# Decay matrices with dt in the exponent and masks on GpSimd, and eight outer convolution taps as ScalarE products added on GpSimd, in a hybrid Conformer/SSD block

## The chip, the cores and the metric

The kernel runs on one core of a Trainium2 chip. The metric is the device time of one execution in microseconds, given as the median of several runs. Engines are named as in the profile: PE is TensorE's matmuls and PEld its weight loads, DVE is VectorE, ACT is ScalarE, POOL is GpSimd, SP is SyncE, whose queue issues all DMAs of this kernel. "L513" is line 513 of the kernel before.

## The reference, cut to what matters

One layer over 512 latent tokens of 1024 channels with a context prefix of 256 tokens. A modulated norm is projected at once into the inputs of two branches.

Branch A is a convolution module: a gated input u, a depthwise convolution of width 31 along grid rows of 64 tokens, LayerNorm, SiLU, a projection:

```python
u = glu[..., :CONV_DIM] * jax.nn.sigmoid(glu[..., CONV_DIM:])
u = dwconv(u.reshape(bsz * n_seg, seg_len, CONV_DIM), lp['conv_dw_w'], lp['conv_dw_b'])
u = jax.nn.silu(layernorm(u.reshape(bsz, l, CONV_DIM), ...))
```

Branch B is a bidirectional Mamba-2 scan with 32 heads of 64 channels in 8 groups, state 128, chunks of 128 tokens. Within a chunk, per head and direction:

```python
cum = jnp.cumsum(dts * a, axis=2)
xdt = x5 * dts[..., None]
seg = cum_t[..., :, None] - cum_t[..., None, :]
decay = jnp.exp(jnp.where(lower, seg, -jnp.inf))
cb = jnp.einsum('bcqgn,bckgn->bcgqk', cs_, bs)
y_diag = jnp.einsum('bcgrqk,bckgrp->bcqgrp', cb[:, :, :, None] * decay, xdt)
```

so the weight of token k in the output at token q is cb[q, k] * exp(cum_q - cum_k) * dt_k for k up to q (backward: from q on), and both directions are added. To this come the states that enter each chunk, decayed by exp(cum). The branches are gated, added and projected, and an MLP with squared ReLU follows.

## The kernel before, in words

Everything is kept channels by tokens, in tiles of 128 channels by 512 tokens, in float32. Each product runs in three passes over high and low parts: `load_w` (L99) brings a weight tile of 128x1024, ScalarE casts the high part (L105, whi), VectorE subtracts (L106, wlo), and `gemm` (L109) does 8 x 3 matmuls of 128x512 (L114 to L116). Raw and split weights have two buffers each.

The program is written as a list; a scheduler orders each engine's queue beforehand by priority (the place in the list) and its own estimate of when things are ready. `later(n)` moves what is traced inside back by n instructions, a negative n forward. On the chip each engine then runs its queue strictly in order.

First come the modulation vectors, the norms and the first products. `dt_part` (L294) finds dt and the running sums cf of dt * a for all heads at once (heads on partitions), exp(cf) (L339), writes both to DRAM (s_cf), and transposes the weights to the chunk's end wg, cf and dt to token-major wgT, cfT, dtT (L350 to L358).

Then follow the eight groups, each with `ssd(g)` beside the projections of the next group, `proj(g+1)`. In `xbc` the product is convolved with 5 taps (ScalarE L370, VectorE L374) and passed through SiLU (L384). `ssd` works thus:
- cps = B^T C for the four chunks (L442), and VectorE multiplies it by a lower and an upper triangle into two tiles cbm (L446).
- B and x are transposed to token-major; x times wgT gives xw (L470), from which the states hst are built (L485 to L498).
- Two halves j of two heads r each. For each head and direction d a DMA (L507) spreads cf and exp(cf) over all partitions into cfb (three buffers). ScalarE makes four pieces Relu(-cf + cfT) (L510, one for each chunk because the bias is a column) and one Exp(-x) over all 512 (L512). VectorE multiplies by cbm (L513). Forward, ScalarE scales the four pieces by dt (L517); backward, VectorE multiplies four pieces by dt and adds them to the forward tile M (L520). Cd = C * exp(cf) (L523) is GpSimd's, but VectorE's for the forward direction of the second head (`DECAYS_V`).
- 24 small products into yps (L532, L536): first the states by Cd, then x by M. VectorE finishes yt (L540, L541), a DMA stores it to s_y, and GpSimd adds up its squares (L548).

Beside groups 0 to 4 one tile of the convolution module runs (`GLU_AT`): `glu` makes the gated input sg (L557, L562), and `taps`, 650 instructions later in priority, does the middle tap with the bias on ScalarE (L569) and the 30 others as `scalar_tensor_tensor` on VectorE (L575), each o += w * shifted u over the tokens that exist; GpSimd adds the finished tiles up into cacc (L580). The last three tiles run behind the groups, then come the gates, the LayerNorm of conv (L644 to L657, results ch and cl), the branch projections, the output projection and the MLP.

Of the kernel before, what the change touches and what calls it, by code (L numbers as in the profile page):

```python
# [24 lines left out]
CK = 31  # L25

# columns of the packed per-channel vectors
# [8 lines left out]
# order of the input projection's 128-column tiles  # L36
# [20 lines left out]
def build(tc, xT, ctxT, cond, crow, wada1, wada2, vecs, hv, cst, w_in, w_co, w_so, w_o, w_1, w_2, outT):  # L57
    nc = tc.nc
    with ExitStack() as es:
# [8 lines left out]
        C = cp.tile([P, 4, P], F32, name="C")  # L68
        ident, ones, mask_f, mask_b = (C[:, i, :] for i in range(4))

# [15 lines left out]
        @contextmanager  # L86
        def later(n):
            """what is traced inside gives way to the next n instructions"""
            tc.cur_priority += n
            yield  # L90
            tc.cur_priority -= n

# [37 lines left out]
        def rsqrt_mean(ps, n, cnt, r=None):  # L130
            """1/sqrt(sum/cnt + EPS) of a sum broadcast over the partitions"""
# [18 lines left out]
        def rsqrt_rows(parts, n, cnt, pool, out=None):  # L150
            """the same of the sum of several tiles, found token by token and then spread over the partitions"""
# [40 lines left out]
        with tc.tile_pool(name="st", bufs=1) as st:  # L192
# [31 lines left out]
            # products of nothing: the tensor engine's clock halves when it idles  # L224
# [52 lines left out]
        nc.sync.dma_start(C[:, 2:], cst[:, 2:])  # L277
# [7 lines left out]
        H2 = 2 * HEADS  # L285
        cfT = cp.tile([P, NCH, H2], F32, name="cfT")
        dtT = cp.tile([P, NCH, H2], F32, name="dtT")
# [6 lines left out]
        def dt_part(ps, pc):  # L294
            conv = bigt("conv")
            # rows: heads forward, the same again, heads backward, the same again; the first of each hold
            # chunks 0 to 2, the second chunk 3 and the context
# [10 lines left out]
            # softplus: max(v, 0) + log1p(u), u = exp(-|v|), log1p(u) = 2 atanh(u / (2 + u))  # L308
# [13 lines left out]
            # running sums within the chunks and within the context, backward ones from the end  # L322
# [15 lines left out]
            nc.vector.tensor_tensor(wg, wg, dt_, ALU.mult)  # L338
            nc.scalar.activation(ecf, cf, AF.Exp)  # L339
# [5 lines left out]
            # step s: chunk s forward, chunk 3 - s backward  # L345
# [4 lines left out]
            for src, dst in ((wg, wgT), (cf, cfT), (dt_, dtT)):  # L350
# [36 lines left out]
        def xbc_first():  # L387
            """the first group's, all of x's part before ctx's"""
# [22 lines left out]

        yacc = acct("yacc")
        cacc = acct("cacc")

# [22 lines left out]
        def ssd(g, Bt, Ct, X, Z):  # L437
            ch = lambda t, c: t[:, c * P:(c + 1) * P]
            # B^T C of every chunk, for both directions
# [3 lines left out]
            cbm = []  # L443
            for m in (mask_f, mask_b):
                t = spool.tile([P, NCH, P], F32, name="cbm", tag=f"cbm{len(cbm)}", bufs=1)
                nc.vector.tensor_tensor(  # L446
                    t, cps.rearrange("p (c q) -> p c q", q=P), m.unsqueeze(1).broadcast_to([P, NCH, P]), ALU.mult)
                cbm.append(t)
            # B by token
# [6 lines left out]
            # x by token, and times what reaches the chunk's end  # L456
# [21 lines left out]
            # states that enter the chunks: step s is chunk s forward, chunk 3-s backward  # L478
# [20 lines left out]
            # outputs of the heads, two to a PSUM tile  # L499
            for j in range(2):  # L500
                yps = py.tile([P, T], F32, name="yps", tag="py")
                Ms, Cs = [], ([], [])
                for r in range(2):
                    for d in range(2):
                        hd = d * HEADS + 4 * g + 2 * j + r
                        cb_ = spool.tile([P, 2, T], F32, name="cfb", tag="cfb", bufs=3)
                        nc.sync.dma_start(cb_, s_cf[hd].unsqueeze(0).broadcast_to([P, 2, T]))  # L507
                        e = (spool if d else tp).tile([P, T], F32, name="e", tag="e" if d else "M", bufs=2 if d else 3)
                        for c in range(NCH):
                            nc.scalar.activation(  # L510
                                ch(e, c), cb_[:, 0, c * P:(c + 1) * P], AF.Relu, bias=cfT[:, c, hd:hd + 1], scale=-1.0)
                        nc.scalar.activation(e, e, AF.Exp, scale=-1.0)  # L512
                        nc.vector.tensor_tensor(e, e, cbm[d].rearrange("p c q -> p (c q)"), ALU.mult)  # L513
                        if d == 0:
                            M = e
                            for c in range(NCH):
                                nc.scalar.activation(ch(M, c), ch(M, c), AF.Copy, scale=dtT[:, c, hd:hd + 1])  # L517
# [47 lines left out]
        def taps(t, sg):  # L565
# [4 lines left out]
            for j in range(CK):  # L570
                d = j - CK // 2
                if d == 0:
                    continue
# [49 lines left out]
        for t in late:  # L623
            q = glu(t, tp, "e")
            with later(LATE_LATER):
                taps(*q)
# [250 lines left out]
```

## Time and profile before

| what | value |
|---|---|
| median of 3 runs | 1263.39 us |
| lowest and highest | 1263.3 and 1267.06 us |
| span of the profiled execution | 1264.2 us |
| PE busy | 1220.7 us (97%) |
| DVE busy | 953.7 us (75%) |
| ACT busy | 667.4 us (53%) |
| POOL busy | 108.9 us (9%), 74 instructions |
| mean granted TensorE clock | 0.991 |

The profile is one execution; its span is 0.8 us above the median of the timed runs. A group of instructions is one line, engine, operation and tile names, with count, busy time and mean duration; behind the second bar stands the engine's idle time just ahead of these instructions and what ended it. Durations on one engine overlap by some tens of ns from one instruction to the next. Matmul ends are modelled, so a waiting PE can look busy.

### The profile page before, as it was taken

To read this page: it belongs to the slowest core of one execution; us is meant where nothing else is said; L and a number is where in the kernel's file an instruction comes from. 1 tells how busy PE (TensorE), PEld (TensorE's weight loads), DVE (VectorE), ACT (ScalarE), POOL (GpSimd) and SP (SyncE) were. 2 spreads that over 40 slices of the span, in tenths; PEclk is the share of its full clock that TensorE was granted. 3 is DMA by queue.
4 is the path that set the end of the run, shared out by engine and by line. 5 is a ranking of instruction groups with operands and counts; after the bars stand their busy time and mean duration, and the time that the engine had idled before them with its cause. 6 is when DMAs were issued, how large, how long until landed. Compare 5 with 4: busy or idle time off the path is not lost.

```text
span 1264.2 us, 17493 instructions
## 1 busy us (share of the span) xinstructions
PE 1220.7 (97%) x6665; PEld 995.6 (79%) x6665; DVE 953.7 (75%) x1567; ACT 667.4 (53%) x1124; POOL 108.9 (9%) x74
## 2 busy tenths in 40 slices
PE   6998999999999899999999999999999999999997
PEld 3786778777787778787888877778998888888886
DVE  6797689999999999998999798885843343443444
ACT  4557888686776748868453452134431331331442
POOL 0001222121020302124000000000000000000000
PEclk8999999999999999999999999999999999999999
DMA  9424363343342424333363357964222333233332
GB/s 363 142 67 133 137 198 128 120 146 106 121 159 93 158 83 147 112 134 117 109 193 126 119 188 258 305 196 153 62 65 86 100 100 92 92 100 101 96 104 67
DMA packets 56260, 169.96 MB, mean 134 GB/s; under 512 B 6640, under 2 KB 9584, under 8 KB 56048
## 3 DMA queue, kind: packets, MB, share of 16 engines
q1 hardware_dynamic: 56176, 168.85, 41.0%
q8 instruction: 52, 0.85, 0.3%
q14 instruction: 32, 0.26, 0.1%
HBM read 162.27 MB, written 6.55 MB: 134 GB/s over the span
## 4 chain that ended last, share of the span: by engine, by line
PE 65%; DVE 20%; DMA 8%; issue 3%; ACT 3%; SPq 0%; POOL 0%; DVEq 0%; ACTq 0%; POOLq 0%
PE ps L114 20%; PE ps L115 19%; PE ps L116 19%; DVE conv L575 5%; DVE wlo L106 3%; DVE Xt L374 3%; DMA aw<-in_wada_dram 2%; DMA cfb<-s_cf 2%; PE yps L536 2%; PE yps L532 2%; PE sps L485 1%; DMA yr<-s_y 1%; DVE aw L675 1%; DMA raw<-in_w_dram 1%; ACT whi L105 1%
## 5 line engine op out<-in xcount | busy, mean ns | idle before, releaser
L105 ACT CAST whi<-raw 128x1024 fp32r<-128x1024 f32 x163 | 170.9, 1049 | 320.6 <-PE ps L115 291.5
L106 DVE TENSOR_TENSOR wlo<-raw,whi 128x1024 fp32r<-128x1024 f32 x163 | 203.8, 1251 | 84.3 <-ACT whi L105 76.1
L114 PE MATMUL ps<-hh,whi 128*128 128x512 f32 x632 | 258.0, 408 | 2.3 <-DVE Xt L374 2.1
L116 PE MATMUL ps<-hh,wlo 128*128 128x512 f32 x632 | 255.4, 404 | 2.3 <-DVE wlo L106 2.2
L115 PE MATMUL ps<-hl,whi 128*128 128x512 f32 x632 | 256.7, 406 | 0.0
L575 DVE SCALAR_TENSOR_TENSOR conv<-sg,V,conv 128x480 f32<-128x480 f32 (+14 forms) x240 | 173.3, 740 | 2.6 <-ACT conv L569 1.1
L114 PEld LDWEIGHTS ps<-hh,whi 128*128 128x128 f32 x632 | 119.4, 189 | 30.8 <-issue 7.2
L116 PEld LDWEIGHTS ps<-hh,wlo 128*128 128x128 f32 x632 | 119.4, 189 | 30.7 <-DVE wlo L106 4.7
L115 PEld LDWEIGHTS ps<-hl,whi 128*128 128x128 f32 x632 | 119.6, 189 | 26.5 <-issue 3.7
L711 DVE SCALAR_TENSOR_TENSOR x<-ps,mod,x 128x512 f32<-128x512 f32 (+1 forms) x48 | 31.7, 660 | 100.1 <-PE ps L116 100.1
L510 ACT ACTIVATE e<-cfb,cfT 128x128 f32<-128x128 f32 x256 | 83.9, 391 | 36.8 <-PE yps L532 17.5
L523 POOL TENSOR_TENSOR Cd<-Ct,cfb 128x512 f32<-128x512 f32 x48 | 72.6, 1518 | 313.0 <-DMA cfb<-s_cf 250.3
L116 PE MATMUL ps<-h2h,wlo 128*128 128x512 f32 (+1 forms) x240 | 89.8, 375 | 0.0
L115 PE MATMUL ps<-h2l,whi 128*128 128x512 f32 (+1 forms) x240 | 89.8, 375 | 0.0
L114 PE MATMUL ps<-h2h,whi 128*128 128x512 f32 (+1 forms) x240 | 89.4, 375 | 0.0
L115 PE MATMUL ps<-gl,whi 128*128 128x512 f32 x224 | 88.4, 395 | 0.0
L114 PE MATMUL ps<-gh,whi 128*128 128x512 f32 x224 | 88.2, 394 | 0.0
L116 PE MATMUL ps<-gh,wlo 128*128 128x512 f32 x224 | 87.9, 392 | 0.0
L374 DVE SCALAR_TENSOR_TENSOR Xt<-ps,V,Xt 128x255 f32<-128x255 f32 (+3 forms) x128 | 74.2, 605 | 3.9 <-ACT Xt L370 3.6
L114 PE MATMUL ps<-hc,whi 128*128 128x256 f32 x184 | 52.5, 285 | 3.1 <-DVE Xt L374 3.1
L115 PE MATMUL ps<-hc,whi 128*128 128x256 f32 x184 | 52.4, 285 | 0.0
L116 PE MATMUL ps<-hc,wlo 128*128 128x256 f32 x184 | 52.1, 283 | 0.0
(259 smaller groups left out, 2417.5 us busy)
## 6 DMA issues: line engine op xcount, KB each, us to landing
raw<-in_w_in_dram SPq DMA_DIRECT2D x81, 512.0 KB, 3.6
cfb<-s_cf SPq DMA_DIRECT2D x64, 512.0 KB, 4.4
raw<-in_w_dram SPq DMA_DIRECT2D x64, 512.0 KB, 3.5
aw<-in_wada_dram SPq DMA_DIRECT2D x64, 256.0 KB, 4.3
ablk<-in_wada_dram SPq DMA_DIRECT2D x16, 512.0 KB, 8.6
raw<-in_w_so_dram SPq DMA_DIRECT2D x16, 512.0 KB, 3.7
s_y<-yt SPq DMA_DIRECT2D x16, 256.0 KB, 2.2
yr<-s_y SPq DMA_DIRECT2D x16, 256.0 KB, 3.6
```

What stands on the lines that cost most here:

```text
L105: nc.scalar.copy(hi, raw)
L106: nc.vector.tensor_tensor(lo, raw, hi, ALU.subtract)
L114: nc.tensor.matmul(ps, lhsT=whi[:, k, :], rhs=rhi[:, k, t0:t1], start=start and k == 0, stop=False)
L115: nc.tensor.matmul(ps, lhsT=whi[:, k, :], rhs=rlo[:, k, t0:t1], start=False, stop=False)
L116: nc.tensor.matmul(ps, lhsT=wlo[:, k, :], rhs=rhi[:, k, t0:t1], start=False, stop=stop and k == KT - 1)
L374: nc.vector.scalar_tensor_tensor(o[:, lo:hi], ps[:, lo + d:hi + d], vcol(V_SCW + 5 * ch + j), o[:, lo:hi], ALU.mult, ALU.add)
L510: nc.scalar.activation(ch(e, c), cb_[:, 0, c * P:(c + 1) * P], AF.Relu, bias=cfT[:, c, hd:hd + 1], scale=-1.0)
L523: (nc.vector if (d, r) in DECAYS_V else nc.gpsimd).tensor_tensor(Cd, Ct, cb_[:, 1, :], ALU.mult)
L532: nc.tensor.matmul(o, lhsT=xt[:, c, hr, :], rhs=ch(Ms[r], c), start=False, stop=True, skip_group_check=True)
L536: nc.tensor.matmul(o, lhsT=hst[:, s, k, hr * 64:hr * 64 + 64], rhs=ch(Cs[k][r], c), start=k == 0 and c == 0, stop=False, skip_group_check= ...
L575: nc.vector.scalar_tensor_tensor(o[:, :, lo:hi], u[:, :, lo + d:hi + d], wv(j), o[:, :, lo:hi], ALU.mult, ALU.add)
L711: nc.vector.scalar_tensor_tensor(x1[:, j, a:b], ps[:, a:b], mod[:, gcol + j, 0:1], x1[:, j, a:b], ALU.mult, ALU.add)
```

## The change

Two edits.

*Decay matrices.* The two masked copies of cps go; one unmasked copy cb is made by ScalarE. The triangle is applied to the exponent: GpSimd's `affine_select` puts -1e30 into cfb (in place) where a token must not count, for each head and direction. dt moves into the exponent as ln(dt): `dt_part` forms bT = ln(max(dt, 1e-18)) - cf in place of cfT and dtT. Then four Exp pieces with bias bT give the finished decay times dt; Relu, the whole Exp and the scalings go. GpSimd adds the backward tile to the forward one, and VectorE multiplies the sum by cb once.

*Convolution.* The eight taps farthest from the middle, d = -15, 15, -14, 14, -13, 13, -12, 12, leave VectorE. For each, ScalarE makes the product w * shifted u into a tile `tap`, and GpSimd adds it to a tile `far`; the first product is written into `far` itself, the rest of which GpSimd sets to zero. When VectorE has done the other 22, GpSimd adds `far` to conv. While the groups run, `far` and `tap` have one buffer each; for the last three tiles they take the three buffers of the tags "Cd" and "M".

```diff
+FAR_TAPS = (0, 30, 1, 29, 2, 28, 3, 27)
+NEVER, DT_MIN = -1e30, 1e-18
+CFB = 3
...
-        C = cp.tile([P, 4, P], F32, name="C")
-        ident, ones, mask_f, mask_b = (C[:, i, :] for i in range(4))
+        C = cp.tile([P, 2, P], F32, name="C")
+        ident, ones = (C[:, i, :] for i in range(2))
...
-        cfT = cp.tile([P, NCH, H2], F32, name="cfT")
-        dtT = cp.tile([P, NCH, H2], F32, name="dtT")
+        bT = cp.tile([P, NCH, H2], F32, name="bT")
...
             nc.vector.tensor_tensor(wg, wg, dt_, ALU.mult)
+            nc.vector.tensor_scalar(dt_, dt_, DT_MIN, None, ALU.max)
+            nc.scalar.activation(dt_, dt_, AF.Ln)
+            nc.vector.tensor_tensor(dt_, dt_, cf, ALU.subtract)
             nc.scalar.activation(ecf, cf, AF.Exp)
...
-            for src, dst in ((wg, wgT), (cf, cfT), (dt_, dtT)):
+            for src, dst in ((wg, wgT), (dt_, bT)):
...
+        def far_tile(name):
+            if not at_end:
+                return spool.tile([P, T], F32, name=name, tag=name, bufs=1)
+            return tp.tile([P, T], F32, name=name, tag="Cd" if name == "far" else "M", bufs=3)
...
-            cbm = []
-            for m in (mask_f, mask_b):
-                t = spool.tile([P, NCH, P], F32, name="cbm", tag=f"cbm{len(cbm)}", bufs=1)
-                nc.vector.tensor_tensor(
-                    t, cps.rearrange("p (c q) -> p c q", q=P), m.unsqueeze(1).broadcast_to([P, NCH, P]), ALU.mult)
-                cbm.append(t)
+            cb = spool.tile([P, T], F32, name="cb", tag="cb", bufs=1)
+            nc.scalar.copy(cb, cps)
...
+                        x3 = cb_[:, 0, :].rearrange("p (c q) -> p c q", q=P)
+                        sign = -1 if d else 1
+                        nc.gpsimd.affine_select(x3, x3, pattern=[[0, NCH], [sign, P]], compare_op=ALU.is_ge,
+                                                fill=never, base=0, channel_multiplier=-sign)
                         for c in range(NCH):
                             nc.scalar.activation(
-                                ch(e, c), cb_[:, 0, c * P:(c + 1) * P], AF.Relu, bias=cfT[:, c, hd:hd + 1], scale=-1.0)
-                        nc.scalar.activation(e, e, AF.Exp, scale=-1.0)
-                        nc.vector.tensor_tensor(e, e, cbm[d].rearrange("p c q -> p (c q)"), ALU.mult)
-                        if d == 0:
-                            M = e
-                            for c in range(NCH):
-                                nc.scalar.activation(ch(M, c), ch(M, c), AF.Copy, scale=dtT[:, c, hd:hd + 1])
-                        else:
-                            for c in range(NCH):
-                                nc.vector.scalar_tensor_tensor(
-                                    ch(M, c), ch(e, c), dtT[:, c, hd:hd + 1], ch(M, c), ALU.mult, ALU.add)
+                                ch(e, c), cb_[:, 0, c * P:(c + 1) * P], AF.Exp, bias=bT[:, c, hd:hd + 1])
+                        es_.append(e)
...
+                    M = es_[0]
+                    nc.gpsimd.tensor_tensor(M, M, es_[1], ALU.add)
+                    nc.vector.tensor_tensor(M, M, cb, ALU.mult)
...
+            far = far_tile("far")
+            f = far.rearrange("p (r w) -> p r w", w=ROW)
+            for i, j in enumerate(FAR_TAPS):
+                d, lo, hi = span(j)
+                uj = u[:, :, lo + d:hi + d]
+                if i == 0:
+                    nc.gpsimd.memset(f[:, :, hi:] if d > 0 else f[:, :, :lo], 0.0)
+                    nc.scalar.activation(f[:, :, lo:hi], uj, AF.Copy, scale=wv(j))
+                    continue
+                q = far_tile("tap")
+                q = q[:, :8 * (hi - lo)].rearrange("p (r w) -> p r w", r=8)
+                nc.scalar.activation(q, uj, AF.Copy, scale=wv(j))
+                nc.gpsimd.tensor_tensor(f[:, :, lo:hi], f[:, :, lo:hi], q, ALU.add)
             for j in range(CK):
-                if d == 0:
+                if d == 0 or j in FAR_TAPS:
                     continue
...
+            nc.gpsimd.tensor_tensor(conv[:, t, :], conv[:, t, :], far, ALU.add)
```

More of the change, by code (lines that the diff above doesn't have):

```diff
@@ L276, in build @@
         nc.sync.dma_start(V[:, V_SNW:], vecs[:, V_SNW:])
-        nc.sync.dma_start(C[:, 2:], cst[:, 2:])
         c_k = lambda k: ctx[k // 2][:, k % 2, :]
@@ L410, in xbc_first @@
             return conv, Bt, Ct, [X0, X1]
+        def far_tile(name):
+            if not at_end:
+                return spool.tile([P, T], F32, name=name, tag=name, bufs=1)
+            return tp.tile([P, T], F32, name=name, tag="Cd" if name == "far" else "M", bufs=3)
+        at_end = []
         yacc = acct("yacc")
         cacc = acct("cacc")
+        never = nc.gpsimd.to_reg(NEVER)
         def proj(g):
@@ L503, in ssd @@
                 for r in range(2):
+                    es_ = []
                     for d in range(2):
                         hd = d * HEADS + 4 * g + 2 * j + r
-                        cb_ = spool.tile([P, 2, T], F32, name="cfb", tag="cfb", bufs=3)
+                        cb_ = spool.tile([P, 2, T], F32, name="cfb", tag="cfb", bufs=CFB)
                         nc.sync.dma_start(cb_, s_cf[hd].unsqueeze(0).broadcast_to([P, 2, T]))
+                        x3 = cb_[:, 0, :].rearrange("p (c q) -> p c q", q=P)
+                        sign = -1 if d else 1
+                        nc.gpsimd.affine_select(x3, x3, pattern=[[0, NCH], [sign, P]], compare_op=ALU.is_ge,
+                                                fill=never, base=0, channel_multiplier=-sign)
                         e = (spool if d else tp).tile([P, T], F32, name="e", tag="e" if d else "M", bufs=2 if d else 3)
@@ L568, in taps, with span @@
             wv = lambda j: vcol(V_DWW + t * CK + j)
+            def span(j):
+                d = j - CK // 2
+                lo, hi = max(0, -d), ROW - max(0, d)
+                return d, lo, hi
             nc.scalar.activation(conv[:, t, :], sg, AF.Identity, bias=vcol(V_DWB + t), scale=wv(CK // 2))
+            far = far_tile("far")
[11 more added lines that the diff above has]
+                nc.gpsimd.tensor_tensor(f[:, :, lo:hi], f[:, :, lo:hi], q, ALU.add)
             for j in range(CK):
-                d = j - CK // 2
-                if d == 0:
+                d, lo, hi = span(j)
+                if d == 0 or j in FAR_TAPS:
                     continue
-                lo, hi = max(0, -d), ROW - max(0, d)
                 nc.vector.scalar_tensor_tensor(
                     o[:, :, lo:hi], u[:, :, lo + d:hi + d], wv(j), o[:, :, lo:hi], ALU.mult, ALU.add)
+            nc.gpsimd.tensor_tensor(conv[:, t, :], conv[:, t, :], far, ALU.add)
             if t == 0:
@@ L621, in gate @@
             nc.scalar.activation(dst[:, t, :], ps, AF.Sigmoid)
+        at_end.append(True)
         for t in late:
@@ L837, in _layout @@
             inp["conv_dw_w"][0].reshape(CK, 8, P).transpose(2, 1, 0).reshape(P, -1)]
-    i = np.arange(P)
-    cst = np.stack([np.eye(P), np.ones((P, P)), i[:, None] <= i[None, :], i[:, None] >= i[None, :]], 1)
+    cst = np.stack([np.eye(P), np.ones((P, P))], 1)
     return {
```

## The prediction

> **What bounds the kernel now.** I read the page's totals first, then the busy time by stage, the matmul groups, and the chain of waits. The columns of the stage table are: stretch, PE (count), PEld, DVE, ACT, POOL, granted clock, DMA share, GB/s.
>
> ```profile
> span 1264.2 us, 17493 instructions
> ```
>
> ```profile
> 100.00:600.00 500.00, 483.13 (x2883) 388.14 (x2882) 457.88 (x748) 375.39 (x718) 100.58 (x66) 0.99 0.40 132
> 600.00:750.00 150.00, 149.82 (x659) 121.41 (x658) 137.10 (x197) 69.69 (x93) 8.14 (x4) 1.00 0.46 145
> ```
>
> The change lies in the stage from 100 to 600 us, where the eight groups of the state-space mixer run, and shortly behind it. There TensorE is recorded idle for 500 - 483.1 = 16.9 us, and VectorE is busy 457.9 of 500 us, that is 92%. In the next 150 us TensorE is full. The modelled ends of matmuls hide more waiting, so I compare one product in two stages:
>
> ```profile
> L114 PE MATMUL ps<-hh,whi 128*128 128x512 f32 x632 | 258.0, 408 | 2.3 <-DVE Xt L374 2.1
> ...
> L114 PE MATMUL ps<-h2h,whi 128*128 128x512 f32 x208 | 80.9, 389 | 0.0
> ```
>
> The same 128x512 pass takes 408 ns among the groups and 389 ns in the MLP, where nothing disturbs it. With 632 of each of three passes (taking the other two like this one) that is 3 x 632 x 0.019 = 36 us of waiting inside "busy". Together with the idle time some 16.9 + 36 = 53 us are the most that this stage can give back. Whom TensorE waits for is in the chain of waits over the same stage:
>
> ```profile
> by line: PE ps L114 13.7%; PE ps L115 13.6%; PE ps L116 13.4%; DVE conv L575 9.3%; DVE Xt L374 6.6%; DVE wlo L106 5.5%; DMA cfb<-s_cf 5.1%; PE yps L536 4.7%; issue 4.6%; PE yps L532 3.6%; PE sps L485 3.4%; DVE e L513 1.6%; DVE xw L470 1.4%;
> ```
>
> PE's own lines add up to 52.4%, so 47.6% is something else. VectorE's lines (conv, Xt, wlo, e, xw) are 24.4% of the stage, about half of that. Of the 53 us I put half, 27 us, down to a VectorE whose queue is full. This apportioning is the weakest step of the reading.
>
> **What leaves VectorE.** The next rows are groups by line: count, busy us, mean ns.
>
> ```profile
> L513 DVE TENSOR_TENSOR e<-e,cbm 128x512 f32<-128x512 f32 x64 | 46.6, 731 | 2.3 <-ACT e L512 2.3
> ...
> L520 DVE SCALAR_TENSOR_TENSOR e<-e,dtT 128x128 f32<-128x128 f32 x128 | 42.6, 358 | 0.2
> ...
> L446 DVE TENSOR_TENSOR cbm<-cps,C 128x512 f32<-128x512 f32 x16 | 10.4, 682 | 1.6 <-PE cps L442 1.4
> ```
>
> The mask products of B^T C (10.4 us), the mask product of each decay (46.6) and the multiply-adds with dt (42.6) go: 99.6 us. In their place each of the 32 pairs of a forward and a backward decay has one product with cb, of L513's shape: 32 x 0.731 = 23.4 us. The outermost taps are these:
>
> ```profile
> L575 DVE SCALAR_TENSOR_TENSOR conv<-sg,V,conv 128x408 f32<-128x408 f32 x16 | 12.6, 786 | 0.0
> ...
> L575 DVE SCALAR_TENSOR_TENSOR conv<-sg,V,conv 128x416 f32<-128x416 f32 x16 | 12.0, 749 | 0.1
> ...
> L575 DVE SCALAR_TENSOR_TENSOR conv<-sg,V,conv 128x400 f32<-128x400 f32 x16 | 11.7, 730 | 0.0
> ...
> L575 DVE SCALAR_TENSOR_TENSOR conv<-sg,V,conv 128x392 f32<-128x392 f32 x16 | 10.6, 661 | 1.2 <-ACT conv L569 1.1
> ```
>
> They sum to 46.9 us over eight channel tiles, 5.9 us for one. Five tiles belong to groups 0 to 4 (29.3 us), three run behind the groups (17.6 us). In the stage VectorE loses 99.6 + 29.3 - 23.4 = 105.5 us of its own work: 457.9 becomes 352.4 us, before what GpSimd adds.
>
> **What ScalarE gains and loses.** Here the columns are min/median/max ns and first and last start.
>
> ```profile
> L510 ACT ACTIVATE e<-cfb,cfT x256: 384/389/418, 112.3 to 601.0; 128x128 f32<-128x128 f32 x128
> ...
> L517 ACT ACTIVATE e<-e,dtT x128: 385/390/435, 119.4 to 600.4; 128x128 f32<-128x128 f32 x128
> L520 DVE SCALAR_TENSOR_TENSOR e<-e,dtT x128: 332/342/992, 123.4 to 604.6; 128x128 f32<-128x128 f32 x128
> L512 ACT ACTIVATE e<-e x64: 612/632/637, 115.3 to 602.0; 128x512 f32<-128x512 f32 x64
> L513 DVE TENSOR_TENSOR e<-e,cbm x64: 673/682/1783, 116.4 to 602.7; 128x512 f32<-128x512 f32 x64
> ```
>
> ```profile
> L613 ACT ACTIVATE yh<-yr,V 128x512 fp32r<-128x512 f32 x16 | 11.1, 724 | 11.6 <-DMA yr<-s_y 11.4
> ```
>
> The 256 pieces stay (Relu becomes Exp, the same form with a bias pointer); the 64 whole Exps (64 x 0.632 = 40 us) and the 128 scalings (128 x 0.390 = 50 us) go. New are eight copies of cps to cb (8 x 0.63 = 5 us) and 64 tap products. They are of L613's kind and somewhat narrower: at most 64 x 0.724 = 46 us, 40 of the 64 in the stage, 29 us. So ScalarE is relieved by 40 + 50 - 5 - 29 = 56 of 375 us, and costs nothing where it waits for nobody. Where it does wait is a rival below.
>
> **What GpSimd takes on.** First a row of how long its 128x512 add or product takes, then one encounter with VectorE.
>
> ```profile
> L523 POOL TENSOR_TENSOR Cd<-Ct,cfb x48: 1264/1304/3853, 112.4 to 594.0; 128x512 f32<-128x512 f32 x48
> ```
>
> ```profile
> 484.86 1.29 POOL L548 TENSOR_TENSOR yacc<-yacc,ysq 128x512 f32<-128x512 f32 x1 [7.49 <-ACT ysq L547]
> ```
>
> ```profile
> 484.76 0.75 DVE L374 SCALAR_TENSOR_TENSOR Ct<-ps,V,Ct 128x510 f32<-128x510 f32 x1
> 485.42 1.28 DVE L513 TENSOR_TENSOR e<-e,cbm 128x512 f32<-128x512 f32 x1
> ```
>
> An undisturbed GpSimd operation takes 1.29 us. In the stage there are 32 adds of the two decays (41 us) and for each of five tiles seven adds about 404 wide (1.29 x 404/512 = 1.02 us) and one of 512: 8.4 us, 42 in all. The 64 mask selections (one input, 128x512, on GpSimd) are in no row. A pass half as dear as the two-input one, 0.65 us, bounds them from below and two such passes, 2.6 us, from above; the nearest row says 1.29, which I take: 83 us. GpSimd goes from 100.6 to 100.6 + 41 + 42 + 83 = 267 us.
>
> The encounter shows the price. L513, median 682 ns, starts beside the GpSimd add, ends 0.55 us after it and takes 1.28 us; it reads two tiles of SBUF. The L374 ahead of it reads PSUM and one tile and keeps its 0.75 us beside the same add. How much such meetings cost in all is the mean against the median:
>
> ```profile
> L575 DVE SCALAR_TENSOR_TENSOR conv<-sg,V,conv 128x480 f32<-128x480 f32 (+14 forms) x240 | 173.3, 740 | 2.6 <-ACT conv L569 1.1
> ```
>
> ```profile
> L575 DVE SCALAR_TENSOR_TENSOR conv<-sg,V,conv x240: 613/684/1770, 198.0 to 706.0; 128x424 f32<-128x424 f32 x10, 128x480 f32<-128x480 f32 x10, 128x432 f32<-128x432 f32 x10, 128x472 f32<-128x472 f32 x9
> ```
>
> ```profile
> L523 DVE TENSOR_TENSOR Cd<-Ct,cfb 128x512 f32<-128x512 f32 x16 | 14.6, 910 | 7.6 <-DMA cfb<-s_cf 5.3 <-POOL Cd L523 1.4 <-issue 0.9
> ```
>
> L575: 240 x 0.056 = 13.4 us; L513: 64 x 0.049 = 3.1; L520: 128 x 0.016 = 2.0; L523 on VectorE, against L513's 682 ns: 16 x 0.228 = 3.6. That is 22 us over the stage's 66 GpSimd operations, 0.33 us each; the weight splits meet it too, and I take 0.4. New in the stage are 64 + 32 + 40 = 136 operations. The 96 of the decays get 0.4 us each (38 us); the 40 tap adds run while VectorE does the same tile's other taps, all of two SBUF inputs, and get 0.7, between 0.4 and their full 1.02: 28 us. VectorE's stage is then 352 + 66 = 418 us instead of 458, a relief of 40 us. The bounds are 352 + 136 x 0.33 = 397 and, with every new operation blocking for its whole length, 352 + 41 + 42 + 83 = 518 us.
>
> The Trainium skill, page "SBUF — State Buffer", section "SBUF: two separate sides", says that the port pair that VectorE and GpSimd share is an exclusive lock, held for the whole instruction, against VectorE instructions with two SBUF inputs. By that rule the upper bound is nearer than my 0.4 us, and it is the second rival; the encounter at 485 us agrees with it, the mean over 66 operations shows how seldom VectorE arrived just then.
>
> **The opening, and what is hidden.**
>
> ```profile
> 98.56 6.00 DMA s_dec<-dec
> 105.50 6.70 DMA cfb<-s_cf
> ```
>
> ```profile
> L512 ACT ACT_TABLE_LOAD x28 | 35.9, 1283 | 0.5
> ```
>
> Before the first decays the chain runs through the dt part and these DMAs. There the change adds a maximum, a logarithm with a table change (1.28 us, once or twice) and a subtraction, less one set of transposes; the first decay then waits for a selection (1.3 us). I charge 3 us (0 to 6). The three late tiles trade 17.6 us of taps for 24 GpSimd operations that VectorE may wait for, about 25 us at worst, so conv ends between 18 us earlier and 8 us later:
>
> ```profile
> L128 DVE TENSOR_TENSOR cl<-conv,ch x8: 684/685/686, 750.7 to 760.4; 128x512 fp32r<-128x512 f32 x8
> ```
>
> ```profile
> L114 PE MATMUL ps<-ch,whi x64: 387/389/396, 801.6 to 848.3; 128*128 128x512 f32 x64
> ```
>
> Its consumer starts 40 us after it is ready, so this costs nothing; only over 40 us late would it. Two fewer constant tiles and the shorter last step before the yps products (one product on VectorE in place of five instructions) I count at nothing beyond the sum.
>
> **The sum.** VectorE's share of the waiting is 27 us. A relief of 40 of 458 us leaves it 84% busy; I let two thirds of its waiting go, 18 us, against 3 us in the opening: -15 us. The profiled execution spans 1264.2 us and the median of the three timed runs is 1263.4 us, 0.8 us less; 1264.2 - 15 - 0.8 gives 1248 us.
>
> **Rivals.**
> 1. *More comes off.* ScalarE's relief counts too, its pieces no longer wait for VectorE (L517, L513), and 40 of the 53 us go: 1263 - 40 + 3 = 1226 us. For it: L513's and L517's steps lie on the path to every yps product. Against: 5.1% of the chain is the DMA of cfb, which stays.
> 2. *The lock eats the relief, slower.* Every new operation blocks VectorE for its whole length: 518 us of work in the stage. At the 96% that VectorE reached at best, that is 540 us, 40 longer: 1303 us. It decides from 106 / 136 = 0.78 us for each new operation, where VectorE is back at 458. For it: the encounter, and that sixteen taps or splits in a row leave no gap. Against: 0.33 us so far.
> 3. *GpSimd becomes the hop that is late, slower.* The decays of a pair now pass GpSimd twice in order, behind products that wait for cfb, and ScalarE's next tap product waits until GpSimd has taken the one before (one buffer), with weight casts and evictions queued behind it. On SyncE's queue a cfb load waits for its slot, and weight loads stand behind it:
>
> ```profile
> SPq L507 <- ACT e L510: 108.7, 33, 10.2
> ```
>
> The slot is now freed one selection later, 64 times 1.3 us on that queue. One operation of 1.5 us (1.29 and a short block) not hidden in each of the 16 half groups is 24 us: 1248 + 24 = 1272 us. With 2.6 us for a selection GpSimd has 351 us of its own work and this gets likelier.
> 4. *VectorE is relieved but was not what TensorE waited for*, or gain and hop cancel: 1263 us, within 0.3%.
>
> **How the numbers follow.** The forecast has 0.33, rival 1 0.21, rival 2 0.17, rival 3 0.17, rival 4 0.12. About 0.3% (4 us) is what a measurement of this kernel can tell from no change. Faster is 0.54, the same 0.12, slower 0.34. The forecast's own range is 1238 to 1258 (bounds of the blocking and of the opening). The range of 8 in 10 takes in rivals 1 and 3 and most of 2: 1222 to 1300 us.
>
> **What would show it.** Right: VectorE's stage at about 420 us busy, L575's mean still under 800 ns, the selections at 1 to 1.5 us, and the 128x512 pass nearer to 395 than 408 ns. Rival 2: means of two-input VectorE rows over 1 us. Rival 3: TensorE or ScalarE rows with a GpSimd releaser of tens of us. The sum is wrong if the stage shortens by under 5 us though VectorE falls to 420, which would be rival 4.

## The result and the profile after

The changed kernel takes 1309.28 us (median of four runs, 1307.22 to 1314.73) against 1265.22 us for the kernel before in the same session: a ratio of 1.0357, 95% interval 1.0329 to 1.0385 (the plain quotient of the two medians, 1.0348, lies inside it). It is slower by 44 us. The prediction was 1248 us, faster, with 1300 us as its upper end; it was wrong, in sign too.

In the kernel after, L118 to L120 are the three passes (L114 to L116 before), L109 and L110 the high and low weight parts, L380 the 5-tap convolution on VectorE, L602 the taps, L533 the product with cb, L525 ScalarE's decay pieces, L541 and L545 the yps products. The execution that was profiled is the longest of the four, 5 us above their median; the spans of the two profiles differ by 48.6 us. First the totals of the page:

```profile
span 1312.8 us, 17408 instructions
...
PE 1227.1 (93%) x6662; PEld 1008.3 (77%) x6662; DVE 918.8 (70%) x1329; ACT 644.7 (49%) x1012; POOL 285.5 (22%) x242
```

and the same two stages as before, with the same columns:

```profile
100.00:600.00 500.00, 458.79 (x2722) 378.70 (x2721) 406.32 (x520) 333.78 (x573) 243.07 (x204) 0.96 0.40 129
600.00:750.00 150.00, 132.64 (x620) 105.80 (x620) 122.25 (x139) 67.54 (x100) 42.02 (x33) 0.95 0.35 106
```

VectorE is down from 457.9 to 406.3 us, as intended. TensorE is busy 24 us less in the first stage (483.1 before) and 17 us less in the next (149.8), and the granted clock fell from 0.99 to 0.96 and from 1.00 to 0.95. All of the loss lies in and just behind these stages, as the first and last start of one product show, first in the kernel after, then in the kernel before:

```profile
L118 PE MATMUL ps<-hh,whi x632: 387/389/988, 38.4 to 756.5; 128*128 128x512 f32 x158
```

```profile
L114 PE MATMUL ps<-hh,whi x632: 387/389/798, 36.3 to 709.4; 128*128 128x512 f32 x158
```

The last of these products starts 47 us later; from there to the end of the span it is 556 us after and 555 before. Where the 47 us lie follows from the last output of a group (VectorE's yt, kernel after and kernel before):

```profile
L550 DVE TENSOR_TENSOR yt<-yt,Z x16: 681/1117/1780, 137.3 to 621.1; 128x512 f32<-128x512 f32 x16
```

```profile
L541 DVE TENSOR_TENSOR yt<-yt,Z x16: 673/683/1345, 140.7 to 607.8; 128x512 f32<-128x512 f32 x16
```

The groups end 13 us later, and the stretch from there to the last product grew by 34 us, from 102 to 135. Part of the 34 us is work: where TensorE waits among the groups, less of the later products (gates and last projections) is done there. The groups of instructions say who pays (count, busy us, mean ns, idle us ahead and its releasers):

```profile
L118 PE MATMUL ps<-hh,whi 128*128 128x512 f32 x632 | 264.8, 419 | 15.3 <-DVE Bt L380 13.8 <-ACT whi L109 1.4
...
L602 DVE SCALAR_TENSOR_TENSOR conv<-sg,V,conv 128x424 f32<-128x424 f32 (+10 forms) x176 | 168.4, 971 | 1.6
...
L533 DVE TENSOR_TENSOR e<-e,cb 128x512 f32<-128x512 f32 x32 | 32.3, 1026 | 12.5 <-POOL e L532 10.0 <-ACT cb L457 2.5
...
L597 POOL TENSOR_TENSOR far<-far,tap 128x400 f32<-128x400 f32 (+3 forms) x56 | 74.4, 1328 | 73.0 <-ACT tap L596 71.6
L529 POOL TENSOR_TENSOR Cd<-Ct,cfb 128x512 f32<-128x512 f32 x48 | 68.0, 1422 | 77.5 <-ACT Ct L390 77.5
L521 POOL TENSOR_SCALAR_AFFINE_SELECT cfb<-cfb 128x512 f32<-128x512 f32 x64 | 50.8, 794 | 135.3 <-DMA cfb<-s_cf 129.5
L532 POOL TENSOR_TENSOR e<-e 128x512 f32<-128x512 f32 x32 | 48.0, 1508 | 33.0 <-ACT e L525 32.9
```

The taps are the main reading. Before, 240 of them cost 173.3 us, 740 ns each; now 176 cost 168.4 us, 971 ns each. Sixty-four taps left VectorE and it got 5 us back. Their median has moved little (684 ns for 30 taps of a tile, now 725 for the wider 22): many run as before, others take twice as long. Which ones do follows from the trace when each tap is set beside what GpSimd ran at the time: the 74 taps that overlap no GpSimd operation take 0.70 us on average and none over 0.74, the 73 that overlap a tap add take 1.22.

```profile
L602 DVE SCALAR_TENSOR_TENSOR conv<-sg,V,conv x176: 650/725/1796, 182.3 to 719.2; 128x424 f32<-128x424 f32 x16, 128x432 f32<-128x432 f32 x16, 128x440 f32<-128x440 f32 x16, 128x448 f32<-128x448 f32 x16
```

The chain of waits over the group stage shows the same from TensorE's side:

```profile
by line: DVE conv L602 14.1%; PE ps L120 8.2%; PE ps L118 7.7%; PE ps L119 7.6%; issue 5.8%; DMA cfb<-s_cf 5.8%; ACT L525 3.9%; DVE wlo L110 3.9%; ACT e L525 3.6%; DVE Bt L380 3.5%; DVE yt L550 3.0%; ACT whi L109 3.0%; PE sps L494 3.0%; DVE
```

The three passes carry 23.5% of the chain, where it was 40.7%, and the taps 14.1%, where it was 9.3% with a third more of them: less of the chain runs over TensorE.

One place shows how. Timelines of the kernel after around 425 us (start, us, engine, instruction, count, idle time ahead), VectorE first, then GpSimd, ScalarE and TensorE:

```profile
420.33 6.86 DVE L602 SCALAR_TENSOR_TENSOR conv<-sg,V,conv 128x464 f32<-128x464 f32 x5
427.12 0.74 DVE L380 SCALAR_TENSOR_TENSOR Bt<-ps,V,Bt 128x510 f32<-128x510 f32 x1
427.78 1.26 DVE L602 SCALAR_TENSOR_TENSOR conv<-sg,V,conv 128x504 f32<-128x504 f32 x1
...
430.28 2.17 DVE L380 SCALAR_TENSOR_TENSOR Bt<-ps,V,Bt 128x511 f32<-128x511 f32 x4
```

```profile
421.79 1.29 POOL L557 TENSOR_TENSOR yacc<-yacc,ysq 128x512 f32<-128x512 f32 x1 [0.52 <-ACT ysq L556]
423.04 1.40 POOL L597 TENSOR_TENSOR far<-far,tap 128x408 f32<-128x408 f32 x1
425.19 1.47 POOL L597 TENSOR_TENSOR far<-far,tap 128x416 f32<-128x416 f32 x1 [0.76 <-ACT tap L596]
427.42 1.09 POOL L597 TENSOR_TENSOR far<-far,tap 128x416 f32<-128x416 f32 x1 [0.75 <-ACT tap L596]
```

```profile
424.47 0.65 ACT L596 ACTIVATE tap<-sg,V 128x416 f32<-128x416 f32 x1 [2.23 <-POOL far L597]
425.02 0.76 ACT L376 ACTIVATE Bt<-ps,V 128x512 f32<-128x512 f32 x1
```

```profile
428.75 0.39 PE L120 MATMUL ps<-hh,wlo 128*128 128x512 f32 x1
432.21 0.77 PE L118 MATMUL ps<-hh,whi 128*128 128x512 f32 x1 [3.07 <-DVE Bt L380]
```

Five taps take 6.86 us; at the median of 0.725 us they are 3.6 us. GpSimd's adds run beside them: four of the five taps end 0.50 to 0.53 us behind the end of a GpSimd add, and the one that begins between two adds takes 0.73 us. The two engines take turns. The eviction of Bt from PSUM is one step on ScalarE (L376) and four on VectorE (L380). The first L380, at 427.12, reads PSUM and one tile and keeps its 0.74 us, but it stands behind the taps in VectorE's queue, and the tap behind it takes 1.26 us beside the add at 427.42. The last of the four is in the group that starts at 430.28. ScalarE's step stands behind a tap product that waited 2.23 us for GpSimd to free `tap`. So two causes meet here, the blocked taps and ScalarE's wait. TensorE waits 3.07 us for the eviction. The first matmul after that wait takes 0.77 us, twice as long as those before it. A wait of the same length stands at 282 us:

```profile
281.66 0.76 PE L118 MATMUL ps<-hh,whi 128*128 128x512 f32 x1 [3.08 <-DVE Bt L380]
```

and windows around that place show TensorE's clock (last three columns: granted clock, DMA share, GB/s):

```profile
281.15:287.95 6.80, 6.05 (x14) 4.30 (x14) 6.80 (x11) 2.13 (x2) 0.00 (x0) 0.50 0.36 93
290.00:296.80 6.80, 6.80 (x43) 6.10 (x42) 6.03 (x8) 2.81 (x4) 2.94 (x2) 1.00 0.31 103
```

The wait of 3.08 us ends at 281.66 us, and in the 6.8 us around and behind its end TensorE is granted half its clock. By the clock column of the stage table, 0.04 x 500 + 0.05 x 150 = 27.5 us of clock is missing, against 0.01 x 500 = 5 us before. The difference, 22 us, is at most what the clock adds to the time, since part of the slow stretches would have been waiting anyway.

Behind the groups the taps of the last three tiles do the same to the weight splits. VectorE, then TensorE, kernel after:

```profile
670.13 6.07 DVE L602 SCALAR_TENSOR_TENSOR conv<-sg,V,conv 128x504 f32<-128x504 f32 x5
676.13 2.00 DVE L110 TENSOR_TENSOR wlo<-raw,whi 128x1024 fp32r<-128x1024 f32 x1
```

```profile
678.18 0.80 PE L120 MATMUL ps<-hh,wlo 128*128 128x512 f32 x1 [3.49 <-DVE wlo L110]
```

The list of waits of the kernel after (total us, times, longest) names both places, and the hop that ScalarE makes:

```profile
ACT tap L596 <- POOL far L597: 40.6, 27, 2.3
...
PEld ps L120 <- DVE wlo L110: 27.5, 19, 4.4
...
PEld yps L541 <- DVE e L533: 15.4, 7, 2.3
...
PE ps L118 <- DVE Bt L380: 13.8, 5, 3.1
```

### The profile page after: what moved, and what is told of

Read it like the earlier page. It is cut to its first block, busy times and chain, and to the rows that moved or that the text cites. A ratio compares the mean times of both kernels' runs of the same rounds, so it can differ in the third digit from the quotient of the medians.

```text
span 1312.8 us, 17408 instructions
## 1 busy us (share of the span) xinstructions
PE 1227.1 (93%) x6662; PEld 1008.3 (77%) x6662; DVE 918.8 (70%) x1329; ACT 644.7 (49%) x1012; POOL 285.5 (22%) x242
## 4 chain that ended last, share of the span: by engine, by line
PE 56%; DVE 22%; ACT 9%; DMA 8%; issue 3%; POOL 1%; SPq 0%; DVEq 0%; ACTq 0%; POOLq 0%
PE ps L120 18%; PE ps L118 18%; PE ps L119 17%; DVE conv L602 7%; DVE wlo L110 3%; DMA aw<-in_wada_dram 2%; DMA cfb<-s_cf 2%; ACT L525 1%; ACT e L525 1%; PE sps L494 1%; ACT whi L109 1%; DVE Bt L380 1%; DVE Xt L380 1%; DVE yt L550 1%; DVE aw L704 1%
## 5 line engine op out<-in xcount | busy, mean ns | idle before, releaser
L109 ACT CAST whi<-raw 128x1024 fp32r<-128x1024 f32 x163 | 170.7, 1048 | 293.6 <-PE ps L119 282.2
L110 DVE TENSOR_TENSOR wlo<-raw,whi 128x1024 fp32r<-128x1024 f32 x163 | 208.9, 1282 | 143.1 <-ACT whi L109 135.2
L118 PE MATMUL ps<-hh,whi 128*128 128x512 f32 x632 | 264.8, 419 | 15.3 <-DVE Bt L380 13.8
L120 PE MATMUL ps<-hh,wlo 128*128 128x512 f32 x632 | 263.5, 417 | 15.6 <-DVE wlo L110 15.6
L602 DVE SCALAR_TENSOR_TENSOR conv<-sg,V,conv 128x424 f32<-128x424 f32 (+10 forms) x176 | 168.4, 971 | 1.6
L120 PEld LDWEIGHTS ps<-hh,wlo 128*128 128x128 f32 x632 | 123.3, 195 | 50.0 <-DVE wlo L110 22.0
L118 PEld LDWEIGHTS ps<-hh,whi 128*128 128x128 f32 x632 | 123.9, 196 | 44.0 <-issue 15.5
L525 ACT ACTIVATE e<-cfb,bT 128x128 f32<-128x128 f32 x256 | 82.9, 392 | 21.2 <-POOL cfb L521 12.6
L597 POOL TENSOR_TENSOR far<-far,tap 128x400 f32<-128x400 f32 (+3 forms) x56 | 74.4, 1328 | 73.0 <-ACT tap L596 71.6
L120 PE MATMUL ps<-h2h,wlo 128*128 128x512 f32 (+1 forms) x240 | 89.8, 375 | 0.0
L118 PE MATMUL ps<-h2h,whi 128*128 128x512 f32 (+1 forms) x240 | 89.4, 375 | 0.0
L118 PE MATMUL ps<-gh,whi 128*128 128x512 f32 x224 | 88.2, 394 | 0.0
L120 PE MATMUL ps<-gh,wlo 128*128 128x512 f32 x224 | 87.9, 392 | 0.0
L529 POOL TENSOR_TENSOR Cd<-Ct,cfb 128x512 f32<-128x512 f32 x48 | 68.0, 1422 | 77.5 <-ACT Ct L390 77.5
L380 DVE SCALAR_TENSOR_TENSOR Xt<-ps,V,Xt 128x510 f32<-128x510 f32 (+3 forms) x128 | 74.3, 605 | 9.0 <-ACT Xt L376 8.4
L521 POOL TENSOR_SCALAR_AFFINE_SELECT cfb<-cfb 128x512 f32<-128x512 f32 x64 | 50.8, 794 | 135.3 <-DMA cfb<-s_cf 129.5
L532 POOL TENSOR_TENSOR e<-e 128x512 f32<-128x512 f32 x32 | 48.0, 1508 | 33.0 <-ACT e L525 32.9
```

The costliest lines, as they stand in the source:

```text
L109: nc.scalar.copy(hi, raw)
L110: nc.vector.tensor_tensor(lo, raw, hi, ALU.subtract)
L118: nc.tensor.matmul(ps, lhsT=whi[:, k, :], rhs=rhi[:, k, t0:t1], start=start and k == 0, stop=False)
L120: nc.tensor.matmul(ps, lhsT=wlo[:, k, :], rhs=rhi[:, k, t0:t1], start=False, stop=stop and k == KT - 1)
L380: nc.vector.scalar_tensor_tensor(o[:, lo:hi], ps[:, lo + d:hi + d], vcol(V_SCW + 5 * ch + j), o[:, lo:hi], ALU.mult, ALU.add)
L521: nc.gpsimd.affine_select(x3, x3, pattern=[[0, NCH], [sign, P]], compare_op=ALU.is_ge, fill=never, base=0, channel_multiplier=-sign)
```

## The experiments

Four theories were open. *Lock*: GpSimd's adds and VectorE's operations with two SBUF inputs exclude each other, and late evictions and splits follow. *Hop*: work stands on the path because it passes GpSimd in order (ScalarE's tap product that waits for the add, the add of the two decays ahead of the yps products). *Decay*: the decay part alone explains the loss. *Clock*: short waits of TensorE cost far more than their length because the clock halves behind them. In the expectations the lock is theory A, the hop of the two decays' add is B and later H, ScalarE's wait is C, a shortage of buffers for the forward decay is I, and the clock is K. Ratios are against the kernel before on the same chip; 0.1% is 1.3 us. The scheduler orders the queues anew for each version. By the traces run 3 has the order of the changed kernel on every engine, and run 8 on TensorE and GpSimd; in run 4 about a tenth of VectorE's instructions stand elsewhere, in run 5 about an eighth of TensorE's products against run 1. What a new order is worth by itself no run shows.

**1. The decay part alone.** All 30 taps back on VectorE.

```diff
-FAR_TAPS = (0, 30, 1, 29, 2, 28, 3, 27)
+FAR_TAPS = ()
-            far = far_tile("far")
...
-            nc.gpsimd.tensor_tensor(conv[:, t, :], conv[:, t, :], far, ALU.add)
```

> The decay part alone; all 30 taps stay on VectorE as in the kernel before. Theory A (the tap adds on GpSimd are the loss: they take turns with VectorE's taps, evictions and weight splits come late, TensorE waits and its clock is halved): 1255 to 1270 us, no wait of TensorE for VectorE's eviction of Bt, granted clock back at 0.985 or more. Theory B (the two decays' add on GpSimd is the late hop): 1290 to 1305 us, and TensorE still waits some 2.3 us for the product with cb in every group.

Measured: 1273.87 us, ratio 1.0094 (1.0069 to 1.0120). That is above the range of theory A and below that of B: the decay part is slower by itself, by 12 us, and the taps cost the rest: 1.0357 - 1.0094 = 2.6%, 33 us. Its group stage:

```profile
100.00:600.00 500.00, 467.48 (x2858) 388.13 (x2857) 425.81 (x574) 319.62 (x545) 205.25 (x162) 0.98 0.40 131
```

VectorE and ScalarE have 32 and 56 us less than before, and TensorE gets 16 us less done. Its waits:

```profile
ACT e L525 <- PE yps L541: 20.0, 7, 7.1
...
PEld yps L541 <- DVE e L533: 18.7, 7, 2.8
...
PE yps L541 <- DVE e L533: 15.7, 7, 2.4
```

and one of these places (GpSimd, VectorE, TensorE):

```profile
249.81 3.26 POOL L532 TENSOR_TENSOR e<-e 128x512 f32<-128x512 f32 x2 [9.10 <-ACT e L525]
```

```profile
251.89 1.73 DVE L533 TENSOR_TENSOR e<-e,cb 128x512 f32<-128x512 f32 x1 [1.17 <-POOL e L532]
```

```profile
253.68 1.09 PE L541 MATMUL yps<-e,xt 128*64 128x128 f32 x14 [2.39 <-DVE e L533]
```

ScalarE's pieces wait for a buffer that the earlier yps products still read; then two adds on GpSimd (3.26 us), then the product on VectorE (1.73 us beside a GpSimd operation), then TensorE, which had run out of other work. GpSimd's add is a link of that path. A wait of the same kind and length 72 us earlier has half the clock behind it; the one at 253.68 has not (TensorE's timeline at 181 us, then a window behind each):

```profile
181.37 1.97 PE L541 MATMUL yps<-e,xt 128*64 128x128 f32 x14 [2.39 <-DVE e L533]
```

```profile
181.00:187.80 6.80, 6.43 (x25) 5.14 (x26) 6.69 (x9) 1.91 (x5) 3.65 (x3) 0.51 0.18 66
253.70:260.00 6.30, 6.30 (x39) 5.29 (x40) 6.19 (x8) 2.13 (x6) 2.99 (x3) 1.00 0.17 66
```

Run 1 has five such waits of 2.39 us. Half the clock came with those that end at 181 and 397 us and not with those at 254, 325 and 469 us.

**2. The change without the 56 adds of far taps.** ScalarE still makes the products; seven of the outer taps are missing from the output.

```diff
-                nc.gpsimd.tensor_tensor(f[:, :, lo:hi], f[:, :, lo:hi], q, ALU.add)
```

> The changed kernel without the 56 adds of the tap products on GpSimd (seven of the eight outer taps are left out of the result); ScalarE's products, the last add and the 22 taps on VectorE stay. Theory A: all of the loss goes and VectorE's relief shows, 1235 to 1255 us, mean of a tap on VectorE back under 750 ns. Theory B: 1290 us or more.

Measured: 1268.43 us, 1.0035 (1.0015 to 1.0055). The adds on GpSimd are worth 1.0357 - 1.0035 = 3.2%, 41 us, though GpSimd was busy only 22% of the span. The relief itself didn't show as expected (1235 to 1255 us): against run 1 VectorE is busy 45 us less (877.8 in place of 923.2 us over the span), and the time falls by 0.6%, 7 us. The taps' row:

```profile
L601 DVE SCALAR_TENSOR_TENSOR conv<-sg,V,conv 128x424 f32<-128x424 f32 (+10 forms) x176 | 140.0, 810 | 1.6
```

Without the adds the 176 taps take 140.0 us in place of 168.4.

**3. The adds without ScalarE's wait.** The add reads u in place of `tap`, so the lock stays and ScalarE's products never wait for the adds; seven far taps go in unweighted.

```diff
-                nc.gpsimd.tensor_tensor(f[:, :, lo:hi], f[:, :, lo:hi], q, ALU.add)
+                nc.gpsimd.tensor_tensor(f[:, :, lo:hi], f[:, :, lo:hi], uj, ALU.add)
```

> The 56 adds stay on GpSimd but read the gated input in place of ScalarE's product (the result of the eight outer taps is wrong by that), so that ScalarE never waits for GpSimd. Theory A in the form that VectorE is blocked: still 1295 to 1312 us, taps on VectorE still over 900 ns. Theory C (ScalarE waits 41 us for its one product buffer, and evictions and weight casts queue behind): 1265 us or less.

Measured: 1301.56 us, 1.0324 (1.0297 to 1.0351). Nearly all of the loss stays; by the ratios, whose intervals overlap, the edit is worth 0.33%, 4 us. But it moves waits more than it takes them away:

```profile
ACT e L525 <- POOL cfb L521: 47.2, 9, 7.7
...
PEld yps L541 <- DVE e L533: 26.5, 7, 4.6
```

ScalarE's pieces wait 47.2 us for selections, where they waited 12.6 in the changed kernel, and TensorE waits 26.5 us for the product with cb in place of 15.4. In exchange its waits for Bt, 13.8 us in the changed kernel, are gone. So the waits at 282 and 432 us needed ScalarE's wait besides the blocked taps, and what that wait costs by itself stays open.

**4. The adds on VectorE.** The same sums; GpSimd keeps only the zeros of `far` and the last add to conv.

```diff
-                nc.gpsimd.tensor_tensor(f[:, :, lo:hi], f[:, :, lo:hi], q, ALU.add)
+                nc.vector.tensor_tensor(f[:, :, lo:hi], f[:, :, lo:hi], q, ALU.add)
```

> The 56 adds are VectorE's. It gets 56 x 0.64 = 36 us of work back, but nothing blocks it for a whole GpSimd add. Theory A: 1255 to 1275 us although VectorE has more work than in the changed kernel. If VectorE's own load decides: 1315 us or more.

Measured: 1278.39 us, 1.0142 (1.0113 to 1.0172). VectorE has 56 adds to make, and the kernel is 2.2%, 27 us, faster than with them on GpSimd, though 3 us above the expected range. ScalarE still waits for the adds, now for VectorE's:

```profile
ACT tap L596 <- DVE far L597: 30.1, 21, 3.1
```

```profile
L602 DVE SCALAR_TENSOR_TENSOR conv<-sg,V,conv 128x496 f32<-128x496 f32 (+10 forms) x176 | 141.9, 814 | 1.5
...
L597 DVE TENSOR_TENSOR far<-far,tap 128x400 f32<-128x400 f32 (+3 forms) x56 | 33.2, 593 | 0.0
```

An add costs VectorE 0.59 us. On GpSimd it costs 1.33 us there and (168.4 - 141.9)/56 = 0.47 us on VectorE's taps alone. So the taps' loss comes in the main from adds that run on GpSimd beside VectorE's taps: 27 us of it goes although ScalarE waits on (30.1 us, 40.6 before the edit). That the adds merely fill GpSimd's queue and make the decays late is not borne out, since TensorE's waits for the product with cb are no longer in the changed kernel than in run 1 (15.4 and 18.7 us). How much of the rest is ScalarE's wait, runs 2 to 4 don't separate.

**5 to 7. The path of the decay part.** On run 1: the add of the two decays on VectorE (5), a fourth buffer for the tag of M (6), both (7).

```diff
-                    nc.gpsimd.tensor_tensor(M, M, es_[1], ALU.add)
+                    nc.vector.tensor_tensor(M, M, es_[1], ALU.add)
```

```diff
-e = (spool if d else tp).tile([P, T], F32, name="e", tag="e" if d else "M", bufs=2 if d else 3)
+e = (spool if d else tp).tile([P, T], F32, name="e", tag="e" if d else "M", bufs=2 if d else 4)
```

> The decay part alone with the add of the two decays on VectorE in place of GpSimd. VectorE gets 32 x 0.69 = 22 us of work more than in the decay part alone (1273.9 us). Theory H (the add's hop over GpSimd makes the product with cb late, and TensorE waits 2.3 to 2.8 us for it in each group and loses clock behind it): 1257 to 1267 us, that wait under 1.5 us. If VectorE's load decides: 1275 to 1285 us.

> The decay part alone with four buffers in place of three for the forward decay tile. Theory I (the last head's Exps of a group start late since all three tiles wait for TensorE's products of the half before, so that all that follows lies on TensorE's path): 1255 to 1267 us, Exps no longer waiting for TensorE. Theory H: 1270 to 1276 us, unchanged.

> The decay part alone with both: the add on VectorE and four buffers. If H and I are both true: 1250 to 1262 us, the best so far. If only one is, as that one alone.

Measured: 1257.76 us, 0.9967 (0.9950 to 0.9983), for the add; 1264.83 us, 1.0024 (1.0012 to 1.0036), for the buffer; 1258.14 us, 0.9978 (0.9963 to 0.9993), for both. Moving the add turns the decay part from 0.9% slower to 0.3% faster, 16 us (the changed order of TensorE's products included), while VectorE gets more to do:

```profile
100.00:600.00 500.00, 478.05 (x2936) 396.10 (x2935) 441.26 (x625) 326.92 (x553) 156.50 (x131) 1.00 0.42 135
```

VectorE is at 441 us here and at 426 in run 1, and TensorE gets 11 us more done at full clock. The buffer is worth 9 us without that, and nothing on top of it, as if both shortened the same path.

**8. Far taps in the five tiles among the groups only.** The three late tiles keep all taps on VectorE.

```diff
+            FAR_TAPS = () if at_end else FAR_GROUPS
```

> The changed kernel with the eight outer taps on ScalarE and GpSimd for the five tiles beside the groups only; the three late tiles do all taps on VectorE. Theory A with the loss split by stage as the traces have it (the late stage waits 21 us more than the work left in it needs): 1285 to 1295 us. If the late stage only inherits a delay from the groups: 1303 us or more.

Measured: 1286.15 us, 1.0197 (1.0178 to 1.0216). Set against run 1 and the full change, the ratios split the loss, in this order of adding the parts: decay part 0.94% (12 us), far taps among the groups 1.03% (13 us), far taps in the three late tiles 1.60% (20 us). The second stage shows the last part:

```profile
600.00:750.00 150.00, 147.26 (x703) 119.46 (x702) 126.71 (x176) 63.45 (x86) 12.07 (x6) 0.99 0.40 123
```

TensorE is busy 147.3 us there at a clock of 0.99, against 132.6 at 0.95 with the late far taps.

**9 and 11. Keeping TensorE busy with zeros.** To price the clock by itself, run 1 got products with a zero weight tile ahead of the yps products that wait: 40 in each group (9), then 20 (11). They add nothing to the sums.

```diff
+ZEROS = 40
...
+        zero = cp.tile([P, 64], F32, name="zero")
+        nc.vector.memset(zero, 0.0)
...
+                    for i in range(ZEROS if k == 2 and j == 1 else 0):
+                        nc.tensor.matmul(yps[64 * (i % 2):64 * (i % 2) + 64, :P], lhsT=zero, rhs=ones,
+                                         start=False, stop=False, skip_group_check=True)
```

> The decay part alone, with 40 small products of zeros (64x128, some 2.2 us, adding nothing to the sums) in TensorE's queue just ahead of the last products of each group, where it waits 2.3 to 2.8 us for the product with cb. Theory K (besides the wait itself, the halved clock behind it is lost; the records show 13.7 us of it between 100 us and the end of the gates in the decay part alone, 3.4 us in the kernel before): the zeros fill the wait, the clock stays up, and 1263 to 1269 us come out against 1273.9 us although TensorE has 17 us more to do. If only the wait counts: 1273 to 1276 us. If the zeros come on top: 1285 us or more.

> As the run before with 20 products of zeros per group in place of 40: in that run the profile recorded 80 passes of 55 ns, 4.5 us per group and not 2.2, so that they overfilled the wait. 20 are 2.25 us, just the wait of 2.3 to 2.8 us in the decay part alone (1273.9 us). Theory K (the halved clock behind the wait is part of the price): 1262 to 1269 us. If only the wait counts: 1273 to 1276 us. If a product of zeros, wherever it stands, comes on top: 1290 us.

Measured: 1307.48 us, 1.0380 (1.0346 to 1.0413), and 1283.8 us, 1.0194 (1.0159 to 1.0229). A zero product is recorded as two passes of 55 ns, so 20 of them in eight groups add 18 us of TensorE time, 40 add 35. With 20 the group stage's clock is back at 0.99, against 0.98 in run 1:

```profile
100.00:600.00 500.00, 467.83 (x3044) 391.82 (x3042) 411.23 (x568) 314.19 (x537) 198.32 (x160) 0.99 0.40 130
```

Yet the kernel is 13 us slower than run 1 by the ratios (1.0194 and 1.0094), less than the 18 us added. TensorE's waits for the product with cb fell from 18.7 to 8.4 us. The clock theory, as priced in the expectations, failed: the filled waits were not worth what the fill cost. The zeros also changed the order of TensorE's other products, so the clock isn't isolated; how much of the half clock is a loss of its own remains open.

**10. What is left of the decay part.** Run 5 with a fourth buffer for cfb.

```diff
-CFB = 3
+CFB = 4
```

> The fastest so far (decay part alone, add on VectorE, 1257.8 us) with four buffers for cfb in place of three. If the loads of cfb still hold up the groups: 1248 to 1255 us. If not: 1256 to 1260 us, no difference.

Measured: 1252.76 us (1249.26 to 1256.33), 0.9932 (0.9910 to 0.9954): the fastest version, ahead of both kernels. The wait of SyncE's queue for a free cfb, in run 5 and then in this run:

```profile
SPq L517 <- ACT e L525: 94.2, 34, 8.2
```

```profile
SPq L517 <- ACT e L525: 80.4, 25, 7.6
```

It shrinks by 14 us only, so that the loads held up the groups agrees with the time but isn't shown step by step. A fourth buffer on the kernel before wasn't tried; so how much of the 0.7% is the new decay form and how much the buffer is told only by run 5, 0.3%, against this run, and their intervals touch.

## Why the prediction was wrong, point by point

**The loads were near.** Predicted for the group stage: VectorE 418 us, GpSimd 267. Measured: 406.3 and 243.1, in a stretch into which a little less of the work falls, since the groups end 13 us later. A selection, taken at 1.29 us, has a median of 0.638 us, just under the lower bound, and a mean of 0.79; four of the 64 take 1.5 to 1.7 us, each beside a weight split of VectorE. ScalarE was forecast 56 us lighter and is 42.

**The step that failed** is "A relief of 40 of 458 us leaves it 84% busy; I let two thirds of its waiting go, 18 us". VectorE fell by 52 us, to 81%, and the time rose by 44 us; the 128x512 pass, forecast nearer to 395 than to 408 ns, takes 419. A busy share says how much an engine has to do, not when it does it. What the runs show in its place: TensorE waits for particular instructions of VectorE (13.8 us for Bt evictions, 18.9 for weight splits, 12.6 for L533; in the kernel before 5.2 for the splits and none for Bt), and each of these got later: in a fixed queue a tap of 1.3 to 1.8 us delays the eviction behind it, however empty the queue is at other times. Run 5 shows it from the other side: 15 us more work on VectorE than in run 1, and 16 us less time. And run 2 against run 1 prices the relief without the tap adds on GpSimd: 45 us less on VectorE, 7 us of time, where the step counts 18 us for 40.

**Where blocking falls was averaged away.** I gave a tap add 0.7 us of blocking, and the size was fair, with 0.47 us measured on the taps alone. But the rows that I averaged came from GpSimd operations that rarely met VectorE. A dense row of taps beside a dense row of adds meets at every instruction, and that row stands in front of the evictions. The forecast that the taps' mean would stay under 800 ns failed: 971. It didn't follow from the sum either: 28 us of blocking on the 110 taps of the five tiles is 0.25 us each, on top of 740 ns. The total of the blocking was foreseen, and what it does to the order was not. The forecast's own range, 1238 to 1258 us, leaves out the upper bound of the blocking, 518 us, though it is said to rest on the bounds.

The Trainium skill, page "SBUF — State Buffer", section "SBUF: two separate sides", has this as an exclusive lock that the first comer of a VectorE operation with two SBUF inputs and a GpSimd operation that reads SBUF holds to its end. The five taps in 6.86 us, in turn with the adds, and the eviction from PSUM that kept its 0.74 us agree with it.

**"so this costs nothing", about the late tiles, was the largest single miss**, 20 us. I asked only who reads conv and found 40 us of slack. I didn't ask what else stands in VectorE's queue behind those taps: the weight splits of the last products, for which TensorE, full before, waited up to 4.4 us.

**Rival 2** (the lock) had the right mechanism and the wrong place: VectorE never came near 518 us, the blocked time hit the order and not the total. Its time, 1303 us, came nearest, but by luck, since the way there was another. **Rival 3** (the hop) was real as well: GpSimd's add of the two decays is worth 16 us (run 5, a new order of the queues included), near its 24, though that was worked out from 16 steps of 1.5 us and run 1 shows seven waits of at most 2.4 us; what ScalarE's wait for the tap adds costs stays open. I held these two for alternatives; they happened together, and that is how the time came out above the range. **Rivals 1 and 4** fell, since the time rose; what ScalarE's relief is worth no run shows by itself.

**The clock was not priced at all.** The forecast let a late VectorE cost TensorE its waiting time. The granted clock halved for some microseconds at the recorded waits of 3.08 and 3.07 us and at some of those of 2.39, and up to 22 of the 47 us could come from it. The Trainium skill, page "TensorE: Matmul & The Clock Gate", Part 1, gives an idle window of about 3.4 us as the condition and half rate as the result; the half rate agrees (0.50), but here a recorded wait of 2.39 us was enough in two of five places of run 1. As runs 9 and 11 failed to isolate it, its share remains open.

The opening, charged with 3 us, can be dismissed: by the two rows of yt, the first output of a group starts 3.4 us earlier than before (137.3 against 140.7).

## What to carry to other kernels

Before moving work from VectorE to GpSimd, ask whether VectorE does operations with two SBUF inputs at that time. Here it did, and the add was paid on both: 1.33 us on GpSimd and 0.47 on VectorE, against 0.59 us on VectorE alone, and the kernel was 27 us faster with the adds there. Before you turn a lighter engine into time, list the instructions of that engine for which the bottleneck waits, and ask of each whether it gets earlier or later. And look at everything queued behind a slowed row, not only at the reader of its result.

## What was not expected of the hardware

A GpSimd selection of 128x512 in float32 takes 0.638 us, half of its two-input add (1.29 us). A TensorE wait of 2.39 us at 181 us of run 1 came with half the clock for 6.8 us, and one of the same length at 254 us with none. And a float32 product with 64 weight columns is recorded as two passes of 55 ns each.
